# Local attention with its scores in two sets of PSUM banks, cache copies moved from the start to the middle, and a reordered tail, in one program

## The chip, the cores and the metric

The program runs on one core of a Trainium2 chip, in one launch. The metric is the device time of one execution in microseconds (us), lower is better. Five engines work side by side, each through its own queue in order: PE (TensorE, the matmuls; PEld is its weight load), DVE (VectorE), ACT (ScalarE), POOL (GpSimd) and SP (SyncE, which here only starts transfers). POOL also starts transfers, through a software queue of its own. All of them meet in SBUF (128 partitions) and in PSUM, whose banks take the matmuls' results.

## The reference

The reference is one inference step of a two-layer decoder on 1024 prompt tokens and 8 single decode tokens, width 1024, all in float32:

```
layer 0: x += norm(mix_A(norm(x)));  x += norm(mlp(norm(x)))    mix_A: gated linear attention + memory attention
shared:  k, v = split(norm(x) @ w_kv)                           4 kv heads of 64
layer 1: x += norm(mix_B(norm(x)));  x += norm(mlp(norm(x)))    mix_B: local attention + memory attention
mix_B:   q, qm = split(h @ w_in_b)
         s = q k^T / 8 + bias(distance), valid for 0 <= distance < 128
         m = max(max(s), sink);  p = exp(s - m) / (sum(exp(s - m)) + exp(sink - m));  o = p v
         decode token: the same over the 127 cached keys and its own
outputs: y of the prompt and of the decode tokens, the GLA states, the last 128 keys and values of the
         prompt, the decode caches shifted by one with the new key and value behind, the memory keys and values
```

The mlp is `square(relu(h @ w_up)) @ w_down` with 4096 hidden units. `norm` is a root-mean-square norm with a gain.

## The kernel before

The residual stream lies feature-major: 8 tiles of 128 features, with the 1032 tokens in three column chunks c = 0, 1, 2 of 384, 384 and 264 (`CH`). A projection in float32 is made of three matmuls on a high and a low part (`wh`, `wl`, `xh`, `xl`), so every weight is loaded (`ws`), cast on ACT (L152) and subtracted on DVE (L153) before PE uses it. The program's stages follow each other: load and norm of x with the first projections and the memory keys and values, linear attention, output projection, mlp of layer 0, projections of layer 1, attention of layer 1, output projection, mlp of layer 1. A scheduler writes each engine's queue once, from the program's order and from priorities (`tc.high_priority(n)` lets work be placed as if it had been written n instructions sooner); an engine never departs from that order.

**The start.** `load_split` (L1019) loads x of a chunk in four tiles `ld` of two feature tiles each. They are slices of one array `xT` of 1032 columns, so a partition's share of a transfer lies in two pieces of 1536 bytes (1056 for chunk 2). At once POOL starts a copy from DRAM to DRAM (L1785, `out_swa_ks`, 1016 KB): the old keys of the decode cache, shifted by one. L1786 does the same for the values at about 63 us. Nothing in the program reads these two results.

**The local attention.** `swa(t, i2)` is one unit: a pair of heads t (of 6) and two blocks of 128 queries, so 24 units. Its steps are: scores (PE, L1726, into a PSUM tile `sA` of two banks, of which the pool holds just one); addition of the bias and row maximum (DVE, L1730, four per unit); exponential with row sum (ACT, L1745, four); multiplication by the reciprocal (DVE, L1751); transposes (PE, L1758, into `sT`); copy to SBUF `pt` (ACT, L1760); product with the values (PE, L1769, into `sf`); copy to `q` (ACT, L1773). The units of t = 0 to 3 lie between the projections of `in_b`, which use two banks `mm`. After `in_b(4)` there are no projections until the output projection, so in the last eight units, (4,0) to (5,3), these two banks are free.

**The decode tokens** are a generator `swa_dec` with five steps: loads and own key; scores against the memory keys (L454, 32 matmuls); transposes and the scores against the cache (L1817); product with the memory values (L454 again) and with the cached values (L1846); copies of the results to `q` (L1862) and `qx` (L492). One step is taken ahead of each unit from (4,2) on. POOL starts its loads: cached keys and values, eight `in_mem_kT`, `vdec`, `dec_sink` and eight `in_mem_v`, the last of which go into the tiles of the memory keys. PE runs in order: a matmul that waits for one of these loads holds all that stand behind it.

**The end.** `down_plain(c)` (L980 on) makes the second projection of the last mlp for chunk c; DVE evicts each result with an addition (L996), `feed_last` squares it on ACT. `Residual.finish` then makes the norm: two last sums (L192), matmuls with a matrix of ones to add over partitions (L198, tile `sf`), logarithm and exponential on ACT (L205, L206), a refinement on DVE (L207 to L209) that leaves the factor `rf`. For each j of four, DVE then multiplies two feature tiles by `rf` (L320) and adds the residual `xall` (L322), and SP stores them to `yT` (L323). The tile `rf` comes from a pool of one buffer, so chunk 2's may be written only after chunk 1's last L320 has read it.

Of the kernel before, what the change touches and what calls it, by code (L numbers as in the profile page):

```python
# [16 lines left out]
P = 128  # L17
# [30 lines left out]
def hybrid_decoder_step(ctx: ExitStack, tc: tile.TileContext, A, O):  # L48
# [30 lines left out]
    xd = dram.tile([P, KT, NT], F32, tag="xd", name="xd")  # L79
# [35 lines left out]
    def first():  # L115
        return tc.high_priority(400)

# [145 lines left out]
    class Residual:  # L263
# [5 lines left out]
        def feed(self, m):  # L269
            if self.last:  # L270
                with first():
                    self.feed_last(m)
            elif m % 2:
                with first() if self.gnext is None else ExitStack():
                    self.sf.add(self.f[:, m - 1 : m + 1, :])
# [11 lines left out]
        def finish(self, bf):  # L287
            c0, n, f = self.c0, self.n, self.f
            rf = rp.tile([P, 384], F32, tag="rf", name=nm("rf"))[:, :n]
            rf2 = rf.unsqueeze(1).to_broadcast([P, 2, n])  # L290
            if self.last:
                with first():
                    self.sf.finish(rf)
            else:
                self.sf.finish(rf, bf)
                hl = xtiles(self.c)
                self.r = rtile(self.c)
# [6 lines left out]
            def load(j):  # L304
                if self.last:
                    got.append(xall[:, 2 * j : 2 * j + 2, :])
                    nc.gpsimd.dma_start(got[-1], self.xsrc[:, 2 * j : 2 * j + 2, c0 : c0 + n])
                    return
                xs = xsp[0].tile([P, 2, 384], F32, tag="xs", name=nm("xs"))[:, :, :n]
                with tc.high_priority(2 * WPRI):  # L310
                    nc.sync.dma_start(xs, self.xsrc[:, 2 * j : 2 * j + 2, c0 : c0 + n])
                got.append(xs)
# [4 lines left out]
            for j in range(4):  # L317
# [3 lines left out]
                if self.last:  # L321
                    TT(f[:, ks, :], f[:, ks, :], xs, ALU.add)  # L322
                    nc.sync.dma_start(O["yT"][:, ks, c0 : c0 + n], f[:, ks, :])  # L323
                    continue
# [5 lines left out]
                nc.scalar.dma_start(xd[:, ks, c0 : c0 + n], f[:, ks, :])  # L330
# [163 lines left out]
    def out_proj(l, make_o, src_pool, st, ff, xsrc, psum=True, oh0=None):  # L494
# [16 lines left out]
        def part(c, ms, pool):  # L511
            n = CH[c][1]
            if c not in FT:
                FT[c] = pool.tile([P, KT, n], F32, tag="f", name=nm("f"))
                R[c] = Residual(c, FT[c], G_MIXPOST + l, xsrc, gnext=G_FFNPRE + l)
# [101 lines left out]
    def mlp(l, X, ff):  # L617
# [45 lines left out]
        def square_mean(c):  # L663
            c0, n = CH[c]
            st = Stats(n, "sx")
            for j in range(4):
                xs = tmp3([P, 2, n])
                nc.sync.dma_start(xs, xd[:, 2 * j : 2 * j + 2, c0 : c0 + n])
                st.add(xs)
# [306 lines left out]
        def down_plain(c):  # L976
            hl = HL[c]
            c0, n = CH[c]
            R[c] = Residual(c, F[c], G_FFNPOST + l, xd, last=(l == 1), floor=X[c][1])
            for m in range(KT):  # L980
# [9 lines left out]
                with first():  # L990
# [48 lines left out]
    def load_x(between, use):  # L1039
        with tc.tile_pool(name="xload", bufs=7, reuse_waits="tile") as xl:  # L1040
            for c in range(3):
# [3 lines left out]
                load_split(xl, hl, A["xT"][:, :, c0 : c0 + n], n, r, G_MIXPRE, (2, 3, 4)[c] * 3 * KT * 384,  # L1045
# [78 lines left out]
    with ExitStack() as sl0:  # L1124
# [479 lines left out]
        with ExitStack() as so:  # L1604
# [30 lines left out]
            X = out_proj(0, make_o0, svp, so, ff, A["xT"], False, oh0)  # L1635
# [4 lines left out]
    with ExitStack() as sl1:  # L1640
# [8 lines left out]
        with ExitStack() as sa:  # L1649
# [63 lines left out]
            def swa(t, i2):  # L1713
# [6 lines left out]
                ps = psS().rearrange("p (j u k) -> p j u k", j=2, u=2)  # L1720
                row = Row()
                for u in range(2):
                    i = 2 * i2 + u
                    for j in range(2):
                        rows = slice(64 * j, 64 * j + 64)
                        row(nc.tensor.matmul(ps[:, j, u, lo[u] :], q[rows, t, i * P : i * P + P],  # L1726
                                             kf[rows, pr, i * P - P + lo[u] : i * P + P], start=True, stop=True))
                for u in range(2):
                    for j in range(2):
                        nc.vector.tensor_tensor_reduce(  # L1730
                            z[:, j, u, lo[u] :], ps[:, j, u, lo[u] :], bias[:, 2 * t + j, lo[u] :], 1.0,
# [43 lines left out]
            def swa_dec():  # L1775
# [8 lines left out]
                nc.gpsimd.dma_start(vc[WIN - 1 : WIN], vdec)  # L1784
                nc.gpsimd.dma_start(O["swa_ks"][:, : WIN - 1, :], A["swa_k_nat"][:, 1:, :])  # L1785
                nc.gpsimd.dma_start(O["swa_vs"][:, : WIN - 1, :], A["swa_v_nat"][:, 1:, :])  # L1786
# [80 lines left out]
            for t in range(6):  # L1867
# [6 lines left out]
                for i2 in range(NB // 2):  # L1874
                    if (t, i2) >= (4, 2):
                        next(dec, None)
# [22 lines left out]
def _arrays(inp):  # L1899
# [8 lines left out]
    a["xT"] = fm(np.concatenate([inp["x_prompt"][0], inp["x_sample"][:, 0]], 0))  # L1908
# [107 lines left out]
```

## Time and profile before

Three runs took 2204.39, 2208.44 and 2211.30 us; the median is 2208.44 us. The profiled execution took 2209.21 us, of which its span is 2207.4 us, so 1.8 us lie around the span. Its mean granted TensorE clock is 0.994.

| engine | busy us | share of the span |
|---|---|---|
| PE | 2152.1 | 97% |
| PEld | 2054.4 | 93% |
| DVE | 1504.0 | 68% |
| ACT | 1061.5 | 48% |
| POOL | 109.4 | 5% |

A row of a timeline reads: start in us, duration in us, engine, line of the kernel, operation, result<-operands, count, and in brackets how long the engine stood idle ahead of it and which engine's work ended that. A row of a table of windows gives the stretch, its length, the busy time of PE, PEld, DVE, ACT and POOL with their counts, the granted clock, the busy share of the DMA engines and the GB/s they moved.

### The profile page before, as it was taken

The page shows a single profiled execution, that of the slowest core. Times are in us where ns is not written, and L with a number is a line of the kernel's source. Part 1 is how long each engine was busy: PE and PEld are TensorE (multiplying, and loading weights), DVE is VectorE, ACT ScalarE, POOL GpSimd, SP SyncE. Part 2 cuts the span into 40 slices and gives each one's busy share as a digit, 9 for nine tenths or more (in the row PEclk, how much of TensorE's full clock was granted, in tenths as well). Part 3 has the DMA queues.
Part 4 walks back from the last instruction along what each step waited for, and adds up shares of the span by engine and source line. Part 5 has one row for each costly group of instructions (what it writes and reads, how often), then busy time and mean ns, then how long its engine had stood idle before and what let it go on. Part 6 is the DMA issues. An engine that isn't in the chain of part 4 may idle for free.

```text
span 2207.4 us, 40137 instructions
## 1 busy us (share of the span) xinstructions
PE 2152.1 (97%) x16250; PEld 2054.4 (93%) x16250; DVE 1504.0 (68%) x2811; ACT 1061.5 (48%) x2071; POOL 109.4 (5%) x123
## 2 busy tenths in 40 slices
PE   7999999999999999999999999799999999999996
PEld 5879999999999999999999778599999999999996
DVE  6656647768877777666478465647887776856557
ACT  6354536557644554334334365646654544433433
POOL 0002000000000002520000000100000000000010
PEclk9999999999999999999999999899999999999998
DMA  5512016543644459574334101324364337635422
GB/s 186 161 63 80 24 64 168 163 131 106 200 157 159 138 196 337 176 256 128 111 95 140 48 20 40 106 73 145 112 219 158 128 138 264 220 112 167 149 88 78
DMA packets 134687, 303.68 MB, mean 138 GB/s; under 512 B 11033, under 2 KB 65489, under 8 KB 134209
## 3 DMA queue, kind: packets, MB, share of 16 engines
q1 hardware_dynamic: 116736, 258.80, 36.0%
q0 software_dynamic: 7824, 29.44, 3.8%
q10 hardware_dynamic: 9936, 12.81, 1.6%
q8 instruction: 129, 2.11, 0.4%
q14 instruction: 62, 0.51, 0.1%
HBM read 213.57 MB, written 89.51 MB: 137 GB/s over the span
## 4 chain that ended last, share of the span: by engine, by line
PE 84%; DVE 4%; ACT 2%; DMA 2%; issue 1%; DVEq 0%; ACTq 0%
PE mm L248 15%; PE mx L248 7%; PE mx L756 6%; PE mx L758 6%; PE mx L757 6%; PE mx L921 4%; PE mx L923 4%; PE mx L922 4%; PE mm L756 3%; PE mm L758 3%; PE mm L757 3%; PE mm L922 2%; PE mm L921 2%; PE mm L923 2%; PE sx L921 1%; PE sf L922 1%
## 5 line engine op out<-in xcount | busy, mean ns | idle before, releaser
L152 ACT CAST wh<-ws 128x512 fp32r<-128x512 f32 (+1 forms) x262 | 188.3, 726 | 319.7 <-DVE ws L605 105.7
L153 DVE TENSOR_TENSOR wl<-ws,wh 128x512 fp32r<-128x512 f32 (+1 forms) x262 | 213.7, 822 | 122.8 <-ACT wh L152 121.7
L756 PE MATMUL mx<-xf,wh 128*128 128x258 f32 x1048 | 297.1, 283 | 0.0
L758 PE MATMUL mx<-xf,wl 128*128 128x258 f32 x1048 | 295.9, 282 | 0.0
L757 PE MATMUL mx<-xf,wh 128*128 128x258 f32 x1048 | 295.7, 282 | 0.0
L248 PE MATMUL mm<-xh,wh 128*128 128x384 f32 (+1 forms) x864 | 282.0, 326 | 0.8 <-ACT xh L152 0.5
L248 PE MATMUL mm<-xh,wl 128*128 128x384 f32 (+1 forms) x864 | 278.9, 323 | 0.0
L248 PE MATMUL mm<-xl,wh 128*128 128x384 f32 (+1 forms) x864 | 278.7, 323 | 0.0
L152 ACT CAST wh<-wr 128x1024 fp32r<-128x1024 f32 x98 | 103.0, 1051 | 315.3 <-PE sx L922 300.3
L153 DVE TENSOR_TENSOR wl<-wr,wh 128x1024 fp32r<-128x1024 f32 x98 | 119.8, 1223 | 173.7 <-ACT wh L152 173.7
L921 PE MATMUL mx<-sa,wh 128*128 128x258 f32 x784 | 221.6, 283 | 1.1 <-DVE aw L594 1.1
L922 PE MATMUL mx<-sa,wh 128*128 128x258 f32 x784 | 220.6, 282 | 0.0
L923 PE MATMUL mx<-sa,wl 128*128 128x258 f32 x784 | 220.5, 282 | 0.0
L757 PEld LDWEIGHTS mx<-xf,wh 128*128 128x128 f32 x1048 | 198.1, 189 | 0.4
L756 PEld LDWEIGHTS mx<-xf,wh 128*128 128x128 f32 x1048 | 197.7, 189 | 0.4
L758 PEld LDWEIGHTS mx<-xf,wl 128*128 128x128 f32 x1048 | 197.9, 189 | 0.0
L248 PEld LDWEIGHTS mm<-xh,wh 128*128 128x128 f32 x864 | 163.0, 189 | 10.8 <-issue 6.3
L248 PEld LDWEIGHTS mm<-xh,wl 128*128 128x128 f32 x864 | 162.6, 188 | 7.4 <-issue 5.4
L248 PEld LDWEIGHTS mm<-xl,wh 128*128 128x128 f32 x864 | 163.2, 189 | 6.5 <-issue 5.5
L921 PEld LDWEIGHTS mx<-sa,wh 128*128 128x128 f32 x784 | 147.5, 188 | 1.6 <-DVE aw L594 1.5
L922 PEld LDWEIGHTS mx<-sa,wh 128*128 128x128 f32 x784 | 148.4, 189 | 0.0
L923 PEld LDWEIGHTS mx<-sa,wl 128*128 128x128 f32 x784 | 148.1, 189 | 0.0
(542 smaller groups left out, 5749.6 us busy)
## 6 DMA issues: line engine op xcount, KB each, us to landing
ra<-awd SPq DMA_DIRECT2D x98, 516.0 KB, 3.9
ws<-in_w_up SPq DMA_DIRECT2D x64, 512.0 KB, 6.1
wr<-in_w_downb SPq DMA_DIRECT2D x56, 512.0 KB, 5.6
awd<-aw SPq DMA_DIRECT2D x26, 1032.0 KB, 6.8
awd<-am SPq DMA_DIRECT2D x28, 774.0 KB, 8.3
ws<-in_w_in_a SPq DMA_DIRECT2D x20, 512.0 KB, 3.6
xd<-f ACTq DMA_DIRECT2D x24, 384.0 KB, 4.8
ws<-in_w_out SPq DMA_DIRECT2D x16, 512.0 KB, 3.5
```

What stands on the lines that cost most here:

```text
L152: nc.scalar.copy(hi, src)
L153: (eng or nc.vector).tensor_tensor(lo, src, f32(hi), ALU.subtract)
L248: mm = nc.tensor.matmul(ps[:M, :n], w_[:, k, :M], x_[:, k, :], start=(i == 0), stop=(i == 3 * KT - 1))
L756: nc.tensor.matmul(ps, wh(k), xh, start=(k == 0), stop=False)
L757: nc.tensor.matmul(ps, wh(k), xl, start=False, stop=False)
L758: mm = nc.tensor.matmul(ps, wl(k), xh, start=False, stop=(k == n - 1))
L921: nc.tensor.matmul(ps, wh[:, q, ms], h, start=(jj == 0 and q == 0), stop=False)
L922: nc.tensor.matmul(ps, wh[:, q, ms], lo, start=False, stop=False)
L923: mm = nc.tensor.matmul(ps, wl[:, q, ms], h, start=False, stop=end)
```

## The change

There are three places. The line numbers of the changed kernel are 3 or 4 higher in the first third, and 9 to 12 higher from `swa` on; elsewhere the five queues hold the same instructions in the same order.

First, the input x and the DRAM copy `xd` of the residual stream become three arrays, one per chunk, so that a tile's share of a partition is one piece. The two shifting copies are put behind the load of `vdec` on POOL's queue, in the middle of the attention.

Second, in the last eight units every second one (i2 = 0 and 2) writes its scores into the two banks `mm`, one per head j, while the others keep `sA`. The decode steps are taken ahead of the units from (4,0) on.

Third, at the end chunk 2's factor has a tile of its own (`r0`), its work has a priority of 4000 in place of 400, and chunk 1's residual additions for j = 1 and 3 go from DVE to POOL.

```diff
...
     def first():
         return tc.high_priority(400)
+
+    def urgent(c):
+        return tc.high_priority(400 if c < 2 else 4000)
...
         def feed(self, m):
             if self.last:
-                with first():
+                with urgent(self.c):
                     self.feed_last(m)
...
-            rf = rp.tile([P, 384], F32, tag="rf", name=nm("rf"))[:, :n]
+            rf = rp.tile([P, 384], F32, tag="r0" if self.last and self.c == 2 else "rf", name=nm("rf"))[:, :n]
             rf2 = rf.unsqueeze(1).to_broadcast([P, 2, n])
             if self.last:
-                with first():
+                with urgent(self.c):
                     self.sf.finish(rf)
...
-                    nc.gpsimd.dma_start(got[-1], self.xsrc[:, 2 * j : 2 * j + 2, c0 : c0 + n])
+                    nc.gpsimd.dma_start(got[-1], self.xsrc[:, 2 * j : 2 * j + 2, :])
...
                 if self.last:
-                    TT(f[:, ks, :], f[:, ks, :], xs, ALU.add)
+                    eng = nc.gpsimd if self.c == 1 and j % 2 else nc.vector
+                    eng.tensor_tensor(f[:, ks, :], f[:, ks, :], xs, ALU.add)
                     nc.sync.dma_start(O["yT"][:, ks, c0 : c0 + n], f[:, ks, :])
...
-                with first():
+                with urgent(c) if l else first():
                     if c < 2:
                         TT(F[c][:, m, :], ps[:, :n], C(m, c)[:, :384], ALU.add)
...
-                load_split(xl, hl, A["xT"][:, :, c0 : c0 + n], n, r, G_MIXPRE, (2, 3, 4)[c] * 3 * KT * 384,
+                load_split(xl, hl, A[f"xT{c}"], n, r, G_MIXPRE, (2, 3, 4)[c] * 3 * KT * 384,
...
-                ps = psS().rearrange("p (j u k) -> p j u k", j=2, u=2)
+                if t >= 4 and i2 % 2 == 0:
+                    ps = [mmps(), mmps()]
+                else:
+                    ps = psS()
+                    ps = [ps[:, :512], ps[:, 512:]]
+                ps = [view(x, [P, 2, 256]) for x in ps]
...
-                        row(nc.tensor.matmul(ps[:, j, u, lo[u] :], q[rows, t, i * P : i * P + P],
+                        row(nc.tensor.matmul(ps[j][:, u, lo[u] :], q[rows, t, i * P : i * P + P],
                                              kf[rows, pr, i * P - P + lo[u] : i * P + P], start=True, stop=True))
...
-                nc.gpsimd.dma_start(vc[WIN - 1 : WIN], vdec)
-                nc.gpsimd.dma_start(O["swa_ks"][:, : WIN - 1, :], A["swa_k_nat"][:, 1:, :])
-                nc.gpsimd.dma_start(O["swa_vs"][:, : WIN - 1, :], A["swa_v_nat"][:, 1:, :])
+                own = nc.gpsimd.dma_start(vc[WIN - 1 : WIN], vdec)
+                for o, src in (("swa_ks", "swa_k_nat"), ("swa_vs", "swa_v_nat")):
+                    shift = nc.gpsimd.dma_start(O[o][:, : WIN - 1, :], A[src][:, 1:, :])
+                    tc.add_manual_dep(shift.ins, own.ins.name, NOSYNC, reason="behind the loads")
...
                 for i2 in range(NB // 2):
-                    if (t, i2) >= (4, 2):
+                    if t >= 4:
                         next(dec, None)
                     swa(t, i2)
```

What is left out of it passes the chunk's own array (`xd[c]`, `xT{c}`) where the slice stood, and cuts the inputs on the host into three arrays of the same values.

PE's queue where the eight units begin (`kf` keys, `q` queries, `sx` decode scores, `sT` transposes, `sf` products with the values) before:

```order
L1790 MATMUL sx_16442<-ident,kf 8x128 x2
L1769 MATMUL sf_16229<-pt_16227,vtok_14265 64x128 x8
L1726 MATMUL sA_16368<-kf,q 128x256 x4
L454 MATMUL sx_16505<-ar_16414,ar_16412 32x256
L1726 MATMUL sA_16461<-kf,q 128x256 x3
L1758 MATMUL sT_16349<-ident,z_16323 128x128 x6
L1726 MATMUL sA_16461<-kf,q 128x256
L1769 MATMUL sf_16358<-pt_16356,vtok_14265 64x128 x6
```

and in the changed kernel:

```order
L1778 MATMUL sf_16231<-pt_16229,vtok_14267 64x128 x8
L1735 MATMUL sA_16479<-kf,q 128x256 x2
L1735 MATMUL mm_16534<-kf,q 128x256
L1735 MATMUL mm_16535<-kf,q 128x256
L1735 MATMUL mm_16534<-kf,q 128x256
L458 MATMUL sx_16416<-ar_16327,ar_16325 32x256
L1735 MATMUL mm_16535<-kf,q 128x256
L1735 MATMUL sA_16609<-kf,q 128x256 x3
L1767 MATMUL sT_16399<-ident,z_16372 128x128 x6
L1735 MATMUL sA_16609<-kf,q 128x256
```

Before, the scores of unit (4,1) (`sA_16368`) and three quarters of those of (4,2) (`sA_16461`) stand ahead of the first transposes of unit (4,0), one tile after the other in the same two banks. Now those of (4,1) in `sA`, of (4,2) in the two `mm` tiles and three quarters of those of (4,3) in `sA` again stand there. The first decode scores (L454, now L458) keep their place beside them.

POOL's queue in the changed kernel around the two copies, with the semaphores that each transfer waits for (DMASW0 to DMASW7 are those of POOL's own transfers, taken in turn, so each transfer waits for the eighth before it):

```order
L1793 DMA ar_16328<-vdec_14257 1x8x256 [waits DMASW3_49]
L1795 DMA out_swa_ks<-in_swa_k_nat 8x2x16256 [waits DMASW4_49]
L1795 DMA out_swa_vs<-in_swa_v_nat 8x2x16256 [waits DMASW5_49]
L1805 MEMSET ar_16328 128x512
L1807 MEMSET ar_16328 128x256
L1818 DMA ar_16325<-in_dec_sink 128x1 [waits DMASW6_49]
L448 DMA ar_16325<-in_mem_v 128x512 [waits DMASW7_49,PE_49]
L448 DMA ar_16325<-in_mem_v 128x512 [waits DMASW0_49]
```

Before, `vdec` was followed by the two MEMSETs, `dec_sink` and the `in_mem_v` loads; the copies now stand ahead of these, and the last two of the eight `in_mem_v` wait for the copies' own semaphores.

DVE's queue at the end (`f_24597` is chunk 1, `f_24601` chunk 2) in the changed kernel:

```order
L195 TENSOR_TENSOR rf_25080<-tq_24969 128x264
L1000 TENSOR_TENSOR f_24601<-mx_25062,acc_21702 128x132
L1000 TENSOR_TENSOR f_24601<-mx_25062,acc_21704 128x132
L326 TENSOR_TENSOR f_24597<-f_24597,xall_24922 128x768
L323 TENSOR_TENSOR f_24597<-f_24597,rf_24913 128x768 x2
L210 TENSOR_TENSOR sf_25082<-sf_25082,rf_25080 128x264
L326 TENSOR_TENSOR f_24597<-f_24597,xall_24922 128x768
L211 SCALAR_TENSOR_TENSOR sf_25082<-sf_25082,rf_25080 128x264
L323 TENSOR_TENSOR f_24597<-f_24597,rf_24913 128x768
L212 SCALAR_TENSOR_TENSOR rf_25080<-sf_25082,rf_25080 128x264
L323 TENSOR_TENSOR f_24601<-f_24601,rf_25080 128x528 x2
```

Before, the sum of chunk 2 (L192, now L195) stood behind chunk 1's fourth multiplication (L320, now L323); now it is ahead of the last two evictions, and chunk 1's leftovers lie between the steps of chunk 2's refinement.

More of the change, by code (lines that the diff above doesn't have):

```diff
@@ L77, in hybrid_decoder_step @@
     nc.vector.memset(oneb, 1.0)
-    xd = dram.tile([P, KT, NT], F32, tag="xd", name="xd")
+    xd = [dram.tile([P, KT, n], F32, tag=f"xd{c}", name=f"xd{c}") for c, (_, n) in enumerate(CH)]
     srd = dram.tile([P, 6, NT], F32, tag="srd", name="srd")
@@ L310, in load @@
                 with tc.high_priority(2 * WPRI):
-                    nc.sync.dma_start(xs, self.xsrc[:, 2 * j : 2 * j + 2, c0 : c0 + n])
+                    nc.sync.dma_start(xs, self.xsrc[:, 2 * j : 2 * j + 2, :])
                 got.append(xs)
@@ L329, in finish @@
                     load(j + ahead)
-                nc.scalar.dma_start(xd[:, ks, c0 : c0 + n], f[:, ks, :])
+                nc.scalar.dma_start(xd[self.c][:, ks, :], f[:, ks, :])
                 if self.gnext is None:
@@ L514, in part @@
                 FT[c] = pool.tile([P, KT, n], F32, tag="f", name=nm("f"))
-                R[c] = Residual(c, FT[c], G_MIXPOST + l, xsrc, gnext=G_FFNPRE + l)
+                R[c] = Residual(c, FT[c], G_MIXPOST + l, xsrc[c], gnext=G_FFNPRE + l)
             for m in ms:
@@ L667, in square_mean @@
                 xs = tmp3([P, 2, n])
-                nc.sync.dma_start(xs, xd[:, 2 * j : 2 * j + 2, c0 : c0 + n])
+                nc.sync.dma_start(xs, xd[c][:, 2 * j : 2 * j + 2, :])
                 st.add(xs)
@@ L978, in down_plain @@
             c0, n = CH[c]
-            R[c] = Residual(c, F[c], G_FFNPOST + l, xd, last=(l == 1), floor=X[c][1])
+            R[c] = Residual(c, F[c], G_FFNPOST + l, xd[c], last=(l == 1), floor=X[c][1])
             for m in range(KT):
@@ L1634, in hybrid_decoder_step @@
                         make_o0(0, oh0)
-            X = out_proj(0, make_o0, svp, so, ff, A["xT"], False, oh0)
+            X = out_proj(0, make_o0, svp, so, ff, [A[f"xT{c}"] for c in range(3)], False, oh0)
         pmd.close()
@@ L1730, in swa @@
                         nc.vector.tensor_tensor_reduce(
-                            z[:, j, u, lo[u] :], ps[:, j, u, lo[u] :], bias[:, 2 * t + j, lo[u] :], 1.0,
+                            z[:, j, u, lo[u] :], ps[j][:, u, lo[u] :], bias[:, 2 * t + j, lo[u] :], 1.0,
                             sinks[:, 2 * t + j : 2 * t + j + 1], ALU.add, ALU.max,
@@ L1906, in fm @@
         return np.ascontiguousarray(x.T.reshape(KT, P, -1).transpose(1, 0, 2))
-    a["xT"] = fm(np.concatenate([inp["x_prompt"][0], inp["x_sample"][:, 0]], 0))
+    x = fm(np.concatenate([inp["x_prompt"][0], inp["x_sample"][:, 0]], 0))
+    for c, (c0, n) in enumerate(CH):
+        a[f"xT{c}"] = np.ascontiguousarray(x[:, :, c0 : c0 + n])
     a["memT"] = fm(inp["mem_prompt"][0])
```

## The prediction

> **What bounds the kernel now.** I began with the page's engine rows and its chain of waits.
>
> ```profile
> span 2207.4 us, 40137 instructions
> PE 2152.1 (97%) x16250; PEld 2054.4 (93%) x16250; DVE 1504.0 (68%) x2811; ACT 1061.5 (48%) x2071; POOL 109.4 (5%) x123
> PE 84%; DVE 4%; ACT 2%; DMA 2%; issue 1%; DVEq 0%; ACTq 0%
> ```
>
> PE is the bound nearly everywhere; 2207.4 − 2152.1 = 55.3 us of the span are without a matmul, and only these, and matmuls at a lower clock, can be saved by an edit that leaves PE's work as it is. The windows and timelines show three clusters of them, which are the three places of the change: the first 20 us, 1379 to 1441 us, and the last 20 us. I go through them in this order; each has its own bound.
>
> **The start.** The table of windows, then ACT's and PE's timelines and the transfers of the first 22 us:
>
> ```profile
> 0.00:10.00 10.00, 1.49 (x4) 0.22 (x4) 1.76 (x6) 3.14 (x4) 0.93 (x5) 1.00 0.79 270
> 10.00:20.00 10.00, 7.30 (x22) 2.72 (x23) 4.21 (x6) 4.56 (x10) 0.00 (x0) 1.00 0.73 246
> 20.00:30.00 10.00, 10.00 (x56) 5.83 (x56) 7.96 (x14) 8.72 (x18) 0.00 (x0) 1.00 0.61 187
> 11.70 1.04 ACT L152 CAST wh<-ws 128x1024 fp32r<-128x1024 f32 x1 [5.05 <-DMA ws<-in_w_in_a]
> 12.70 1.50 PE L1172 MATMUL mg<-ld,vtok 128*32 128x384 f32 x4 [6.38 <-DMA ld<-in_xT]
> q0 software_dynamic: 48, 1.04, 11.7%
> out_swa_ks<-in_swa_k_nat POOLq DMA_DIRECT2D x1, 1016.0 KB, 9.3
> ```
>
> In the first 20 us PE works 8.8, and the releasers of both long waits are transfers, the first weight and the second tile of x. The software queue's one transfer is the key copy; it took 11.7% of 16 engines over 22 us, so 0.117 × 22 = 2.6 us of all of them, ahead of or beside these loads. Taken away, ws and ld land up to 2.6 us sooner. The transfer engines were busy for 0.79 of the first 10 us and not for all of it, so 0.79 × 2.6 = 2.1 us is the share that I count; the longer pieces of x (the same bytes) add perhaps 0.4, an estimate between nothing and the 6.38 us of PE's wait. Term: **2.5 us**. Low bound 0.5: the casts of x on ACT and DVE could be the next limit, as ACT is 8.72 of 10 busy from 20 to 30. High bound 5: both waits 5.05 and 6.38 gone nearly whole. From 20 us on PE has no idle time, so what it gains is kept. `out_swa_vs` leaves the stretch at 63 us where PE is full anyway: nothing.
>
> **The middle.** PE's waits from 1378.8 to 1441.5 us, the stretch from the last projection to the output projection without a hole, and windows of it:
>
> ```profile
> PE sT L1758 <- DVE z L1751: 4.2, 4, 1.6
> PE sf L1769 <- ACT pt L1760: 3.2, 5, 1.2
> PE sA L1726 <- DVE sm L1730: 2.4, 3, 2.0
> PE sT L1758 <- DVE sm L1828: 2.0, 1, 2.0
> ...
> 1378.80:1441.50 62.70, 49.51 (x431) 32.92 (x430) 44.12 (x162) 38.87 (x108) 10.55 (x21) 0.89 0.29 96
> 1390.00:1400.00 10.00, 9.68 (x63) 5.36 (x64) 5.25 (x20) 5.27 (x18) 0.54 (x1) 0.59 0.13 45
> 1387.95 2.07 PE L1726 MATMUL sA<-kf,q 64*128 64x256 f32 x6 [1.95 <-DVE sm L1730]
> 1383.94 1.13 PE L1726 MATMUL sA<-kf,q 64*128 64x256 f32 x8
> ```
>
> No engine is full: PE 49.5, DVE 44.1 and ACT 38.9 of 62.7 us. PE stands because each unit is a chain (scores, maximum, exponential, normalising, transposes, copy, values) and the next unit's scores must wait until DVE has read the one `sA`. Of that kind is the wait of 1.95 us at 1387.95; behind it the clock is 0.59 and six score rows take 2.07 us where eight took 1.13.
>
> What each edit brings:
> - Two sets of score banks: the waits of `sA` on L1730, **2.4 us**, go. Low 0, if they return one unit later.
> - The slow stretch: at full clock its 9.68 us of matmuls would be 0.59 × 9.68 = 5.7, so up to 4.0 us. It follows the wait that goes, but a new one can bring it back; I take **2.5**.
> - With the scores of three units ahead, DVE and ACT find the next unit's work sooner, and the waits on `z` and `pt`, 4.2 + 3.2 = 7.4 us, shrink. The last units keep theirs, having nothing left to hide them. I take **3**; bounds 0 and 5.
> - New: the copies of the decode queries (L1803) and the result copy of unit (4,0) now stand on DVE and ACT behind unit (5,0)'s maxima and exponentials, so PE's L1817 and the values of (4,1), queued behind it, wait. The nearest row is the 2.0 us that PE stood for L1828: **−2**.
> - Decode steps two units sooner in the program move few rows on PE: both groups of L454 stand by unit (4,0)'s and (5,0)'s transposes as before. Nothing, as long as their loads have landed (below).
>
> Sum 2.4 + 2.5 + 3 − 2 = **5.9 us**. Bounds: −2 (only the new wait) and 4.0 + 2.4 + 5 = 11.4.
>
> The clock: by the Trainium skill, "TensorE: Matmul & The Clock Gate", Part 1, the clock halves after an idle window of about 3.4 us. The row shows half rate behind a wait of 1.95 us, shorter than that page's window, so the trace agrees in the halving but not in the length; by the page's length the 2.5 would have to come from something else and the middle would be 3.4.
>
> Where the copies go, POOL and its transfers:
>
> ```profile
> 1379.72 3.19 POOL L444 DMA_DIRECT2D ar<-in_mem_kT  x6
> 1387.70 0.57 POOL L1808 DMA_DIRECT2D ar<-in_dec_sink  x1 [2.89 <-DMA ar<-in_swa_kT]
> 1400.24 3.71 POOL L444 DMA_DIRECT2D ar<-in_mem_v  x7 [1.87 <-PE sx L454]
> ar<-in_swa_kT POOLq DMA_DIRECT2D x1, 1016.0 KB, 11.8
> ar<-in_mem_kT POOLq DMA_DIRECT2D x8, 256.0 KB, 9.3
> ar<-in_mem_v POOLq DMA_DIRECT2D x8, 256.0 KB, 4.6
> 1416.03 0.42 PE L454 MATMUL sx<-ar,ar 128*32 128x256 f32 x3
> ```
>
> The copies go out from about 1387.7, when in_swa_kT's landing lets POOL on. At 9.3 us each, side by side, they land by about 1399. In this stretch the engines move 45 GB/s from 1390 to 1400, so there is room. Queued behind on POOL's queue are dec_sink and the eight in_mem_v; these issued at 1397.8 to 1404 and landed by 1409, and PE read them at 1416. Five to seven us of slack cover the delay: nothing, with the price of a lost cover under the rivals.
>
> **The end.** Timelines of PE, DVE and ACT from 2187 us:
>
> ```profile
> 2193.45 1.25 PE L198 MATMUL sf<-rf,ones 128*128 128x264 f32 x2 [5.62 <-DVE rf L192]
> 2194.49 1.97 PE L198 MATMUL sf<-t,ones 128*128 128x264 f32 x4
> 2188.51 1.81 DVE L320 TENSOR_TENSOR f<-f,rf 128x768 f32<-128x768 f32 x2
> 2190.24 1.82 DVE L322 TENSOR_TENSOR f<-f,xall 128x768 f32<-128x768 f32 x2
> 2192.96 0.43 DVE L192 TENSOR_TENSOR rf<-tq 128x264 f32<-128x264 f32 x1
> 2188.62 0.42 ACT L280 ACTIVATE t<-f 128x264 f32<-128x264 f32 x1 [0.30 <-DVE f L996]
> 2196.91 0.42 ACT L206 ACTIVATE rf<-rf 128x264 f32<-128x264 f32 x1
> 2197.37 0.44 DVE L207 TENSOR_TENSOR sf<-sf,rf 128x264 f32<-128x264 f32 x1 [3.11 <-ACT rf L206]
> 2198.78 1.33 DVE L320 TENSOR_TENSOR f<-f,rf 128x528 f32<-128x528 f32 x2
> 2202.50 1.32 DVE L322 TENSOR_TENSOR f<-f,xall 128x528 f32<-128x528 f32 x2
> ```
>
> Before, DVE finishes chunk 1 (0.87 us per operation, from (2190.24 − 2188.51) / 2) up to L192, and only then PE sums chunk 2: 5.62 us of wait, then 3.0 us of cold matmuls, and 3.11 us of wait on DVE. Then eight operations of 0.62 us, 5.0 in all, to 2203.8, and 3.6 us of store and closing.
>
> Now L192 stands ahead of the last evictions, so the sums are done by about 2189.6 (last square of ACT at 2189.0, then two rows), ACT's two operations of 0.42 each by 2190.5. Of chunk 1, DVE has L322, L320 twice (to 2191.2), and between the refinement's three steps of 0.45 L322 and L320 once each: 5 × 0.87 + 3 × 0.45 = 5.7 from 2188.6, to 2194.3, and with the eight of chunk 2 to 2199.3. That would be 4.5 us less. But two additions of chunk 1 now run on POOL, and this is what two-operand work on POOL costs beside DVE:
>
> ```profile
> 880.05 19.65 POOL L237 TENSOR_TENSOR wf<-wf,gains 128x1024 f32<-128x1024 f32 x1 [4.64 <-DMA wf<-in_w_kv]
> 908.78 1.89 POOL L237 TENSOR_TENSOR wf<-wf,gains 128x1024 f32<-128x1024 f32 x1 [4.18 <-DMA wf<-in_w_in_b]
> 849.26 2.93 DVE L153 TENSOR_TENSOR sa<-ra,sa 128x1032 fp32r<-128x1032 f32 x1
> 896.72 1.22 DVE L153 TENSOR_TENSOR sa<-ra,sa 128x1032 fp32r<-128x1032 f32 x1
> 900.70 1.23 DVE L153 TENSOR_TENSOR wl<-wr,wh 128x1024 fp32r<-128x1024 f32 x1 [2.75 <-ACT wh L152]
> ```
>
> The same POOL operation takes 1.89 us alone and 19.65 when DVE works without a hole until 897.9, and then ends 1.8 us behind that. At 849.26 it is DVE that waits, 2.93 us in place of 1.22. The two exclude each other while both read two operands from SBUF. The Trainium skill says so in "SBUF — State Buffer", "Who interferes with whom": such a pair shares a read interface, and whoever starts first holds it for the whole instruction; the trace agrees.
>
> An addition of 768 takes 1.89 × 768/1024 = 1.4 us on POOL. The steps of the refinement read `sf` from PSUM, so POOL gets in beside L207 and beside L209, and DVE's next operation waits for the rest, 1.4 − 0.45 = 1.0 us each time. 2199.3 + 2 × 1.0 = 2201.3, against 2203.8: term **2.5 us**. High bound 4.5 (no exclusion), low −0.5: POOL gets in only when DVE is done at 2199.3, its two additions end at 2202.1, and chunk 2's four stores, queued behind chunk 1's last on SP, go out from there instead of 2200.7.
>
> **Sum.** 2.5 + 5.9 + 2.5 = 10.9 us from 2209.2, so 2198.3; I say **2198**. The profiled execution is 0.8 us above the median of the three runs, which themselves lie 7 us apart.
>
> **Rivals.**
> 1. The middle gives nothing: the wait moves from `sA` to L1817 and the values of (4,1), the slow clock returns behind it, and only start and end stay: 2209.2 − 5.0 = 2204. For it: each unit's chain is as long as before, and the waits on `z` and `pt` are larger than those on `sA`. Against it: DVE has 18.6 us of idle time there to be filled.
> 2. POOL is shut out at the end, as at 880: 2.5 + 5.9 − 0.5 = 7.9, so 2201. For it: that row. Against it: the refinement steps read PSUM, and 849 shows that POOL can win between two operations of DVE.
> 3. All comes: middle 11.4, end 4.5, start 2.5, 2191. For it: the waits and slow rows are all there to be had. Against it: the row at 849, and the order of the copies.
> 4. Slower: the copies hold up in_mem_v. If they run one after the other (9.3 each would be 1406.3; with in_swa_kT's 11.8 for the second, 1408.8) and the eight loads then at the pace of in_mem_kT, of which six went out from 1379.7 to 1382.9 and landed by about 1382.9 + 9.3 = 1392.2, so 12.5 us for six and 16.6 for eight, the last lands at 1425. PE reaches the second L454 group at about 1410 in the forecast, so it stands 15 us with the rest of (5,0) to (5,3) behind it, and 4.0 us more at the slow clock: middle 5.9 − 19 = −13, with start and end 5.0, in all 8 us slower, 2217. It decides once in_mem_v lands more than 11 us behind PE's need. Against it: the light load of 45 GB/s and the slack above.
>
> **Chances.** Forecast 0.55, rival 1 0.22, rival 2 0.10, rival 3 0.08, rival 4 0.05. A measurement here can tell about 0.3%, 6.6 us: faster means below 2201.8. Of the forecast nine tenths lie there, with rival 3 and half of rival 2: 0.50 + 0.08 + 0.05, and a little of rival 1: 0.65. Within 0.3%: 0.30. Slower: 0.05. The range runs from near rival 3 to past rival 1, since start and middle can both fall to their low bounds: 2189 to 2208; the forecast's own is 2194 to 2202.
>
> **What would show it.** Start: the first L152 (now L155) at about 9 instead of 11.70, and PE's first full window sooner. Middle: no wait of scores on L1730's successor, the granted clock of the ten us behind 1388 near 1, a wait of about 2 us at the decode scores, the output projection's steady run starting 6 us sooner counted from the last projection. A wait of L458 on in_mem_v would speak for rival 4. End: sums by 2190 counted with the old origin, DVE operations of 0.87 us stretched to about 1.9 beside two POOL rows of 1.4; POOL rows of 5 us or more that end behind DVE's last would be rival 2. I am wrong if the middle's stretch of 62.7 us does not shrink by at least 3, or if the end is not shorter by 1.5.

## The result

The changed kernel takes 2192.48 us (median of 6 runs, 2189.01 to 2196.33), the kernel before 2204.66 us (6 runs, 2203.33 to 2211.30): a ratio of 0.9935, with a 95% interval of 0.9921 to 0.9948. It is faster by 0.65%. The forecast was 2198 us in a range of 2189 to 2208. The profiled execution of the changed kernel took 2194.83 us, its span 2193.0 us, 14.4 us less than before.

To place these 14.4 us I compare the same matmul in both traces. All kernels here have 16250 of them. Four marks cut the span: the last projection matmul ahead of the eight units; matmul number 10501, which lies in the output projection behind them and is the same one in every kernel; the last matmul of the second mlp projection; the end of the span.

| us | to the last projection | middle | output projection and mlp | end | span |
|---|---|---|---|---|---|
| before | 1378.56 | 81.16 | 727.83 | 19.88 | 2207.43 |
| changed | 1375.29 | 73.92 | 726.25 | 17.55 | 2193.01 |
| difference | −3.27 | −7.24 | −1.58 | −2.33 | −14.42 |

The start, from the changed kernel's table of windows and the timelines of ACT and PE:

```profile
0.00:10.00 10.00, 3.10 (x9) 0.58 (x10) 3.28 (x8) 5.74 (x8) 0.20 (x4) 1.00 0.81 292
10.00:20.00 10.00, 10.00 (x40) 4.68 (x40) 6.48 (x12) 6.27 (x15) 0.00 (x0) 1.00 0.46 165
7.40 1.04 ACT L155 CAST wh<-ws 128x1024 fp32r<-128x1024 f32 x1 [1.03 <-DMA ws<-in_w_in_a]
8.40 1.50 PE L1176 MATMUL mg<-ld,vtok 128*32 128x384 f32 x4 [2.34 <-DMA ld<-in_xT]
```

The first weight is there at 7.40 instead of 11.70, and PE's second group starts at 8.40 instead of 12.70, 4.3 us sooner. In this pair of profiles about 1 us of that is lost on the way to the eight units.

The middle, from PE's waits between 1375 and 1433 us, a window, and the timelines of POOL, DVE and PE:

```profile
PE sf L1827 <- issue: 1.9, 1, 1.9
PE sf L1778 <- ACT pt L1769: 1.2, 1, 1.2
PE sT L1767 <- DVE z L1760: 0.9, 2, 0.6
PE sA L1735 <- DVE sm L1739: 0.7, 1, 0.7
...
1400.00:1410.00 10.00, 8.50 (x89) 5.22 (x81) 4.22 (x17) 2.34 (x6) 0.00 (x0) 0.53 0.01 2
1386.51 0.54 POOL L1805 MEMSET ar<- 128x512 f32 x1
1386.97 0.33 POOL L1807 MEMSET ar<- 128x256 f32 x1
1391.59 4.26 POOL L448 DMA_DIRECT2D ar<-in_mem_v  x8 [3.78 <-PE sx L458]
1397.93 0.16 DVE L1756 TENSOR_TENSOR sm<-sm,sm 128x4 f32<-128x4 f32 x1 [2.06 <-ACT z L1754]
1398.23 1.00 DVE L1813 COPY ar<-q 64x12 f32<-64x12 f32 x8
1399.73 1.18 PE L1827 MATMUL sf<-ar,ar 128*32 128x128 f32 x32 [1.86 <-issue]
```

The wait of scores on the maxima fell from 2.4 to 0.7 us; those of the transposes on `z` and of the products on `pt` fell from 7.4 to 2.1. A new one is longest, 1.86 us at the decode scores (L1827, L1817 before), and behind it the clock is 0.53 for ten microseconds. The waits that go and those that come are the forecast ones; why the new one stands there is the subject of the experiments.

The end, from the timelines of PE, DVE and POOL:

```profile
2176.18 1.32 PE L201 MATMUL sf<-t,ones 128*128 128x264 f32 x4
2178.25 2.29 POOL L326 TENSOR_TENSOR f<-f,xall 128x768 f32<-128x768 f32 x1 [58.00 <-DVE f L323]
2179.14 2.22 DVE L326 TENSOR_TENSOR f<-f,xall 128x768 f32<-128x768 f32 x1
2182.70 1.79 POOL L326 TENSOR_TENSOR f<-f,xall 128x768 f32<-128x768 f32 x1 [2.16 <-issue]
2182.94 2.74 DVE L323 TENSOR_TENSOR f<-f,rf 128x528 f32<-128x528 f32 x2
2188.08 1.31 DVE L326 TENSOR_TENSOR f<-f,xall 128x528 f32<-128x528 f32 x2
```

The sums are done within 2.0 us of the last matmul's start instead of 8.9. Beside each of POOL's two additions one DVE row is stretched: 2.22 us where 0.95 is usual, and 2.74 for a pair that takes 1.33.

### The profile page after: what moved, and what is told of

Its sections match the earlier page's. It is cut to its first block, busy times and chain, and to the rows that moved or that the text cites. A ratio compares the mean times of both kernels' runs of the same rounds, so it can differ in the third digit from the quotient of the medians.

```text
span 2193.0 us, 40134 instructions
## 1 busy us (share of the span) xinstructions
PE 2148.5 (98%) x16250; PEld 2053.3 (94%) x16250; DVE 1506.6 (69%) x2809; ACT 1060.4 (48%) x2071; POOL 107.8 (5%) x125
## 4 chain that ended last, share of the span: by engine, by line
PE 91%; DVE 3%; ACT 2%; DMA 2%; issue 1%; POOL 0%; SPq 0%; DVEq 0%; ACTq 0%
PE mm L251 17%; PE mx L251 8%; PE mx L760 6%; PE mx L762 6%; PE mx L761 6%; PE mx L925 4%; PE mx L927 4%; PE mx L926 4%; PE mm L762 3%; PE mm L760 3%; PE mm L761 3%; PE mm L925 2%; PE mm L926 2%; PE mm L927 2%; PE sx L925 1%; PE sf L926 1%
```

## The experiments

The table collects every profile, cut at the same marks. "Time" is the ratio to the kernel before with its interval, where it was timed.

| kernel | first mark | middle | mlp | end | span | time |
|---|---|---|---|---|---|---|
| before | 1378.56 | 81.16 | 727.83 | 19.88 | 2207.43 | 1 |
| changed | 1375.29 | 73.92 | 726.25 | 17.55 | 2193.01 | 0.9935 (0.9921 to 0.9948) |
| first place alone | 1373.20 | 88.11 | 726.24 | 19.89 | 2207.44 | 1.0004 (0.9992 to 1.0015) |
| second place alone | 1378.59 | 66.07 | 726.28 | 19.87 | 2190.81 | 0.9939 (0.9919 to 0.9958) |
| third place alone | 1375.80 | 82.19 | 726.29 | 17.54 | 2201.82 | 0.9988 (0.9975 to 1.0001) |
| changed, additions on DVE | 1375.13 | 72.69 | 726.28 | 16.42 | 2190.53 | 0.9940 (0.9917 to 0.9963) |
| changed, copies late | 1375.61 | 67.63 | 726.29 | 17.55 | 2187.06 | 0.9913 (0.9900 to 0.9927) |
| both of these | 1372.07 | 68.87 | 727.78 | 16.41 | 2185.13 | 0.9905 (0.9888 to 0.9921) |
| changed, copies behind dec_sink | 1374.07 | 67.84 | 726.30 | 17.56 | 2185.76 | one run, 2187.55 us |
| arrays alone | 1377.11 | 77.03 | 727.15 | 19.88 | 2201.17 | one run, 2202.99 us |
| banks alone | 1378.02 | 70.69 | 726.27 | 19.88 | 2194.86 | 0.9964 (0.9950 to 0.9978) |
| decode sooner alone | 1378.56 | 87.85 | 727.86 | 19.89 | 2214.16 | 1.0043 (1.0030 to 1.0056) |

The end repeats within 0.02 us, so differences there can be read to a tenth. The first mark varies by about 3 us between kernels that are alike up to it (third place alone: 1375.80, before: 1378.56), and the mlp lies between 726.2 and 727.9; there a difference of 1 to 3 us tells nothing by itself.

The middle varies most. Before, third place alone and arrays alone have the same order of instructions in it on PE, DVE, ACT and POOL, and it took 81.16, 82.19 and 77.03 us. The records of the granted clock show what differs. In the next table "PE idle" is the time of the middle without a matmul and "half clock" the time for which the granted clock was 0.5. "At most" is half of PE's busy time in it, the most that the half clock can have cost.

| us in the middle | whole | PE idle | half clock | at most |
|---|---|---|---|---|
| before | 81.16 | 13.2 | 13.7 | 6.4 |
| third place alone | 82.19 | 12.9 | 17.1 | 8.1 |
| arrays alone | 77.03 | 14.6 | 0 | 0 |
| first place alone | 88.11 | 14.1 | 34.1 | 14.0 |
| decode sooner alone | 87.85 | 14.9 | 20.5 | 10.1 |
| banks alone | 70.69 | 8.2 | 3.4 | 1.7 |
| changed | 73.92 | 7.6 | 10.2 | 4.4 |
| changed, additions on DVE | 72.69 | 7.6 | 6.8 | 3.0 |
| second place alone | 66.07 | 4.0 | 0 | 0 |
| changed, copies late | 67.63 | 4.4 | 3.4 | 1.7 |
| both of these | 68.87 | 4.3 | 6.8 | 3.4 |
| changed, copies behind dec_sink | 67.84 | 4.9 | 0 | 0 |

PE's idle time holds within 2 us among kernels that are alike in the middle; the half clock does not. It shows in the whole time too: the kernel before ran 50 more times beside the experiments, and its runs with a mean granted clock of 0.996 took 2202.7 us on average (9 runs), those with 0.991 took 2211.1 (4 runs).

### The first place alone

```diff
-    xd = dram.tile([P, KT, NT], F32, tag="xd", name="xd")
+    xd = [dram.tile([P, KT, n], F32, tag=f"xd{c}", name=f"xd{c}") for c, (_, n) in enumerate(CH)]
...
+                    tc.add_manual_dep(shift.ins, own.ins.name, NOSYNC, reason="behind the loads")
```

> The kernel before with the first place of the change alone: the three arrays of x and of its DRAM copy, and the two shifting copies behind the load of vdec. My theory, from the changed kernel's traces: PE's steady run starts 4.3 us sooner, about 1 us of that is lost again between 80 and 100 us, so the last projection before the eight units ends about 3.3 us sooner (1375.3 instead of 1378.6) and the whole takes 3 us less. The copies, now in the middle, cost nothing there: from the last projection to the output projection's steady run it stays at 62.7 us. Rival: the copies hold up dec_sink or in_mem_v in the order of before, the middle grows by 2 us or more and the whole gains 1 us or less.

The start came (PE's matmul 251 at 53.65 instead of 58.36 us, the first mark 5.4 us sooner), and all of it was lost again: the middle took 88.11 us instead of 81.16, and the ratio is 1.0004. The rival was right in its size. PE's waits in the middle of this kernel:

```profile
PE sA L1726 <- DVE sm L1730: 4.4, 4, 2.1
PE mm L248 <- DVE xl L153: 2.4, 1, 2.4
PE sf L1818 <- issue: 1.5, 1, 1.5
...
1402.18 1.33 PE L1726 MATMUL sA<-kf,q 64*128 64x256 f32 x8 [2.14 <-DVE sm L1730]
1407.09 1.94 PE L1818 MATMUL sf<-ar,ar 128*32 128x128 f32 x32 [1.48 <-issue]
```

None of them is a wait for a transfer, so the rival's reason, copies that hold up dec_sink or in_mem_v, is not seen. PE's idle time is 14.1 us where it was 13.2. What is longer is the time at the half clock, 34.1 us instead of 13.7; the decode scores take 1.94 us instead of 1.08 there. All ten runs show it, with mean clocks of 0.989 to 0.992 where the 20 runs of the kernel before beside them had 0.991 to 0.996. The order of instructions in the middle is another one than before, on PE, DVE and ACT: the decode scores start 33.9 us behind the first mark instead of 26.9.

### The second place alone

```diff
+                if t >= 4 and i2 % 2 == 0:
+                    ps = [mmps(), mmps()]
...
-                    if (t, i2) >= (4, 2):
+                    if t >= 4:
```

> The kernel before with the second place alone: every second one of the last eight units has its scores in the two projection banks, and the decode steps begin two units sooner. Theory: from the last projection to the output projection's steady run the changed kernel took 55.6 us where before took 62.7, and this part alone gives that, 7 us less in all, with the wait of about 1.9 us at the decode scores. Rival: a part of the 7 us comes from the copies or the earlier start, and this part alone gives 4 or less.

The middle took 66.07 us, 15.1 less than before and 7.9 less than in the changed kernel. Both theory and rival are wrong: nothing of the 7 us came from the copies, and the kernel that has them in the middle is 7.9 us longer there. The kernel with this place alone is as fast as the whole change. Waits and windows:

```profile
PE sA L1731 <- DVE sm L1735: 1.2, 1, 1.2
PE mm L248 <- DVE xl L153: 0.7, 1, 0.7
PE sf L1822 <- issue: 0.5, 1, 0.5
PE sf L1774 <- ACT pt L1765: 0.5, 1, 0.5
PE sT L1763 <- DVE z L1756: 0.4, 1, 0.4
...
1390.00:1400.00 10.00, 9.45 (x120) 6.22 (x118) 9.73 (x47) 9.14 (x35) 4.55 (x9) 1.00 0.41 129
1400.00:1410.00 10.00, 9.90 (x113) 6.50 (x111) 8.87 (x39) 6.68 (x22) 0.00 (x0) 1.00 0.30 111
```

From 1390 to 1410 PE is busy 19.4 of 20 us at the full clock, where the changed kernel had 0.53 in the second half; the decode scores wait 0.5 us instead of 1.86.

### The third place alone

```diff
-            rf = rp.tile([P, 384], F32, tag="rf", name=nm("rf"))[:, :n]
+            rf = rp.tile([P, 384], F32, tag="r0" if self.last and self.c == 2 else "rf", name=nm("rf"))[:, :n]
...
+                    eng = nc.gpsimd if self.c == 1 and j % 2 else nc.vector
```

> The kernel before with the third place alone: chunk 2's factor in a tile of its own, its work with priority 4000, and two of chunk 1's additions on POOL. Theory: from the end of the last matmul of the second mlp projection to the end of the span it takes 17.2 us instead of 19.6, so 2.3 less, and nothing else moves. Rival: the 1.7 us that the changed kernel gained between the output projection and the last matmul come from the new priorities, and this kernel is 4 us faster.

The end took 17.54 us, 2.34 less, as the theory has it. The mlp was 726.29 us as in the changed kernel, but the second place alone, which has none of the new priorities, shows 726.28 too. So the 1.58 us of the mlp do not belong to the change: in the profile of before PE waits 0.75 and 0.31 us there, at about 1860 us, and such waits are in some profiles and not in others. The time agrees in size, 0.9988, though its interval reaches 1.

### The changed kernel with the additions on DVE

```diff
-                    eng = nc.gpsimd if self.c == 1 and j % 2 else nc.vector
-                    eng.tensor_tensor(f[:, ks, :], f[:, ks, :], xs, ALU.add)
+                    TT(f[:, ks, :], f[:, ks, :], xs, ALU.add)
```

> The changed kernel with chunk 1's four residual additions all on DVE again. Theory, that POOL and DVE exclude each other: in the changed kernel two operations of DVE are longer by 1.3 and 1.4 us, 2.7 in all, beside POOL's rows of 2.29 and 1.79 us; two additions of 0.87 us on DVE cost 1.7, so this kernel is 0.9 us faster at the end than the changed one. Rival, that POOL's work is free beside DVE and the long rows have another cause: it is 1.7 us slower at the end, with the long rows still there.

The end took 16.42 us, 1.13 less than with POOL. The additions on DVE and what stands beside them:

```profile
2177.80 0.95 DVE L325 TENSOR_TENSOR f<-f,xall 128x768 f32<-128x768 f32 x1
2179.00 0.95 DVE L325 TENSOR_TENSOR f<-f,xall 128x768 f32<-128x768 f32 x1
2183.18 1.32 DVE L323 TENSOR_TENSOR f<-f,rf 128x528 f32<-128x528 f32 x2
```

With POOL idle no row is stretched. So at the end the new order and the tile of its own are worth 3.46 us (19.88 − 16.42), and moving two additions to POOL costs 1.13 of them. In the whole time 1 us is below what these runs can tell.

### The copies late, and both improvements

```diff
+            for o, src in (("swa_ks", "swa_k_nat"), ("swa_vs", "swa_v_nat")):
+                shift = nc.gpsimd.dma_start(O[o][:, : WIN - 1, :], A[src][:, 1:, :])
+                tc.add_manual_dep(shift.ins, zset[0].ins.name, NOSYNC, reason="behind the last memset")
```

Here `zset[0]` is the memset of unit (5,0), the last of POOL's work for the attention; the lines at the load of vdec are gone.

> The changed kernel with the two shifting copies behind POOL's memset for unit (5,0), thus behind all loads of the decode tokens, where POOL has nothing else to do until the residual loads of the last mlp. Theory: in the changed kernel the copies cost the middle some 8 us (it gained 15 us without them and 7 with them), because what stands behind them on POOL's queue was planned and done later. Here the middle takes 48 us instead of 55.6, as with the second place alone; start and end stay as in the changed kernel (about 4 and 2.3 us less than before); in all 20 to 22 us less than before. Rival: the gain of the second place alone hung on the copies being at the start, by the phase in which its loads arrive, and this kernel is no faster than the changed one.

> The same with chunk 1's additions all on DVE: theory 1.1 us less than with the copies late and the additions on POOL, the end at 16.4 us instead of 17.5, in all 21 to 23 us less than before. Rival: the two do not add up, and it is the same as that kernel within its interval.

With the copies late the middle took 67.63 us, 6.3 less than in the changed kernel, and the time is 0.9913 (0.9900 to 0.9927), against 0.9935 (0.9921 to 0.9948) of the changed kernel. The two intervals overlap by 0.0006, so the times alone only just part the two. In the middle the kernels that have the copies ahead of the memsets (73.92 and 72.69 us) lie above those that don't (66.07 to 68.87). The saving in span is 20.4 us, as forecast. With the additions on DVE as well the median is 2185.81 us, the ratio 0.9905 (0.9888 to 0.9921), the fastest of all kernels here, about 1% below before. That it beats the version with the late copies alone shows at the end (16.41 against 17.55 us), while the two intervals of the time overlap.

### The copies behind dec_sink

```diff
-                for o, src in (("swa_ks", "swa_k_nat"), ("swa_vs", "swa_v_nat")):
-                    shift = nc.gpsimd.dma_start(O[o][:, : WIN - 1, :], A[src][:, 1:, :])
-                    tc.add_manual_dep(shift.ins, own.ins.name, NOSYNC, reason="behind the loads")
...
-                nc.gpsimd.dma_start(dsink, A["dec_sink"])
+                own = nc.gpsimd.dma_start(dsink, A["dec_sink"])
+                for o, src in (("swa_ks", "swa_k_nat"), ("swa_vs", "swa_v_nat")):
...
```

> The changed kernel with the copies behind dec_sink and ahead of the in_mem_v loads, so that their traffic stays in the same stretch but the two memsets and dec_sink are ahead of them. Theory: the cost comes from the memsets (and the decode scores that need them), so the decode scores stand beside the transposes of (4,1) again, and the middle takes 51 us or less; what remains is the later in_mem_v. Rival: the traffic of 2 MB read and written itself, or the waits of in_mem_v behind it, is the cost, and the middle stays at 55 us or more.

The middle took 67.84 us: the theory's side, and better than its number. The timelines of POOL, DVE and PE:

```profile
1378.93 0.54 POOL L1802 MEMSET ar<- 128x512 f32 x1
1384.27 0.60 POOL L1817 DMA_DIRECT2D out_swa_ks<-in_swa_k_nat  x1 [0.89 <-DMA ar<-in_mem_kT]
1389.67 1.03 DVE L1810 COPY ar<-q 64x12 f32<-64x12 f32 x8
1391.26 1.08 PE L1827 MATMUL sf<-ar,ar 128*32 128x128 f32 x32 [0.51 <-issue]
```

The copies go out at the same time as in the changed kernel (1384.3 here, 1384.45 there), ahead of the same eight in_mem_v, and the middle is as short as in the kernels that have them elsewhere (66.07 to 68.87). So neither their traffic nor the waits of in_mem_v are the price. What differs is the order in which all engines' queues were written. Here DVE copies the decode queries (L1810) at 1389.67; in the changed kernel (its rows are under the result) it makes the copies (L1813) 8.6 us later, at 1398.23, after standing 2.06 us for ACT's exponentials, though both memsets were done by 1387.3. The memsets were ready 10.9 us before; they are not what the copies waited for. The copies stand late in DVE's queue, behind unit (5,0)'s maxima, because the scheduler writes the queues by what it reckons; with the two large copies ahead of the memsets on POOL it put everything that needs the memsets further back, on DVE, ACT and PE. That the reckoning did so is what I infer from the orders, and no run shows it; that the order differs, and that the memsets were ready long before their use, is in the rows.

### The arrays alone

The first place without the three lines on the copies.

> The kernel before with the three arrays of x and of its copy alone; the shifting copies stay at the start and at 63 us. Theory: of the 4.3 to 4.7 us by which PE's steady run started sooner with both, the copy's traffic is the larger part (2.6 us of all engines), so this one gives 1 to 2 us. Rival: the longer pieces are the larger part, 3 us or more.

PE's matmul 251 starts at 57.03 us. The five kernels with the old start have it between 57.34 and 58.36, so the arrays alone are worth 0.3 to 1.3 us, which one profile doesn't tell from nothing; PE's second group, at 12.07, lies within theirs (11.97 to 13.43). The six kernels with the whole first place have matmul 251 between 51.80 and 54.01, so the larger part is the copies', as the theory has it. The one run's 2202.99 us at a clock of 0.996 is what the kernel before takes at that clock. More telling is the middle. It has the order of before and took 77.03 us, 4.1 less:

```profile
1386.49 1.13 PE L1726 MATMUL sA<-kf,q 64*128 64x256 f32 x6 [1.95 <-DVE sm L1730]
1390.00:1400.00 10.00, 8.85 (x97) 5.59 (x94) 7.82 (x35) 6.38 (x20) 4.60 (x9) 1.00 0.45 135
```

The same wait of 1.95 us, and behind it the clock is 1.00 and six score rows take 1.13 us, where in the profile of before it was 0.59 and they took 2.07. So the slow stretch does not follow from the wait alone; the same program position can have it or not. Without it the middle is 4.1 us shorter although PE's idle time is 1.4 us longer; the most that before's 13.7 us at half clock can have cost is 6.4.

### The two halves of the second place

The two edits of the second place shown above, one each.

> The kernel before with the score banks alone: every second one of the last eight units in the two projection banks, the decode steps still ahead of (4,2) and later units. Theory: the banks carry most of the 13 to 15 us of the second place, since they take away what made a unit's scores wait for the one before: 8 us or more of it. Rival: without the decode steps moved, the decode work piles up behind the last units, and the banks alone give 4 us or less.

> The kernel before with the decode steps two units sooner alone, all scores in the one tile of two banks. Theory: it gives the rest, 3 to 6 us, as the decode matmuls fill PE's waits earlier and the last units have none behind them. Rival: with one tile for the scores PE's waits on it stay, and it gives nothing or is slower.

The banks alone gave 10.5 us of the middle's 15.1 and 0.9964 of the time: the theory. Against the 77.03 us of the same order at full clock it is 6.3; PE's idle time fell by 5.0. The decode steps alone made it slower, 87.85 us and 1.0043: the rival. PE's waits with the decode steps sooner and one tile of scores:

```profile
PE sT L1758 <- DVE z L1751: 8.4, 4, 3.4
...
1389.29 1.13 PE L1758 MATMUL sT<-ident,z 128*128 128x128 f32 x6 [3.37 <-DVE z L1751]
1390.00:1400.00 10.00, 9.55 (x92) 5.67 (x91) 4.74 (x24) 4.11 (x14) 2.02 (x4) 0.67 0.15 45
```

PE stands 3.37 us for the normalised rows of one unit, 8.4 in four waits where before had 4.2, and the clock is down behind the first. PE's idle time is 1.7 us longer than before in all, and 20.5 us instead of 13.7 are at half clock. I take it that with one score tile, decode work that is planned earlier is put ahead of units that then have no scores ready; which of its rows does that was not taken apart, and so it is not shown. The two edits need each other: −10.5 and +6.7 alone, −15.1 together.

## Why the prediction was right or wrong

**The time** was forecast 0.3% too high in the median, 5.5 us, inside the range; 4.5 of them come from the base, since the forecast counts from the profiled 2209.2 us and the median before is 2204.66; the direction and the size of the gain (10.9 forecast; 14.4 in the profile, 12.2 between the medians) were right. The end came out for the reasons told, the start for its reason with a size too small, the middle for other reasons.

**The start, 2.5 us.** The reason held: PE waited for the first weight and the second tile behind the copy. The term was too small: 4.3 us at PE's first groups and 3.3 at the first mark, and over all profiles, five with the old start and six with the new, the mean difference is 4.7 us at matmul 251 and 3.7 at the first mark. The step that was mis-sized is the 2.1 us for the copy, made of its share of the engines' time and a further discount of 0.79. With the arrays alone matmul 251 stood at 57.03 us, and with the copies gone as well 3.0 to 5.2 us sooner. Why that is more than the copy's 2.6 us of all engines stays open. The 0.4 for the arrays is not shown: they gave 0.3 to 1.3, within what such profiles differ.

**The middle, 5.9 us.** The sum came out at 7.2, by errors that cancelled; that it is near 5.9 is luck.
- The step "the copies ... nothing, with the price of a lost cover under the rivals" was wrong. Where the score banks are there they cost 4 to 8 us (73.92 and 72.69 against 66.07 to 68.87), of which about 3 are PE's idle time and the rest goes with the clock. In the old order they cost 7 us in the profiles (88.11 against 81.16), and there it is nearly all the half clock; the 1.0004 of the time says that they took back what the start had gained. I had looked for the cost in the landing of in_mem_v. That was on time as I had worked out: issued from 1391.6 to 1395.9, landing 4.2 us later, read by PE at 1409.9. Rival 4 had the right cause and the wrong mechanism: not a late transfer, but other engines' queues written in another order.
- The step "**−2**" for the new wait was right in place and size (1.86 us at L1827), but I took it as a price of the score banks. It is the copies' price: without them there the decode scores wait 0.5 us.
- The terms for the banks were too small. For the waits 2.4 + 3 = 5.4 stood against 9.2 us of idle time that PE lost in the second place alone (13.2 to 4.0). For the slow clock 2.5 stood against up to 6.4, all of which the profile of before happened to have and this one did not. The two together account for the 15.1 measured. The waits on `z` and `pt` shrank from 7.4 to 0.9 in the second place alone, not by 3: the end of the eight units did not keep its waits, as I had thought.
- "Decode steps two units sooner in the program move few rows on PE ... Nothing" was wrong. I read it off the changed kernel's order, which had the copies in it. Alone that edit costs 6.7 us, beside the banks it brings 4.6 (70.69 − 66.07), 4.2 of it in PE's idle time.

**The clock.** I took 2.5 of 4.0 us for the slow stretch, as if it hung on the wait of 1.95 us. The arrays alone show the same wait and no slow stretch, and the clock's records show why. In each of the twelve traces all changes of the granted clock lie on one grid of 3.41 us, to within 4 ns, and the grid lies otherwise against the program in each. In the profile of before the whole wait falls into one piece of that grid, 1384.53 to 1387.94 us, in which PE was busy 33% of the time, and the clock falls at its end. With the arrays alone the grid cuts the wait in two: PE is busy 56% of the piece from 1382.30 to 1385.72 and 74% of the next, and the clock stays. Over all twelve traces, every piece at full clock in which PE is busy 43% or less is followed by half clock, no piece with 59% or more is, and between these both occur. So my step went by the length of the wait, where PE's share of a piece of the grid decided, and with it the chance of where the grid lies. The Trainium skill, "TensorE: Matmul & The Clock Gate", Part 1, says that the window in which activity is judged runs freely and does not begin with the kernel's work. The grid in these traces agrees with it.

**The end, 2.5 us.** 2.33, and by the steps as told: the sums ready early, POOL in beside the refinement's steps twice, two DVE rows longer by 1.3 and 1.4 us (I had 1.0 each), POOL's rows 2.29 and 1.79 us where I had 1.4 alone. Had I worked out the sum without POOL, 4.5 us, and set the two additions' 1.7 against it, I would have seen that moving them is worth nothing there: measured 3.46 without POOL, 2.33 with it.

**The rest, 1.58 us** between the output projection and the last matmul, was in no term, and is no effect of the change: kernels with none of the new priorities show it, and the fastest kernel does not.

**Rivals.** Of rival 1 the wait at L1817 and the slow clock behind it happened as told (0.53 from 1400 to 1410), but the middle gained 7 us all the same, since the second place was worth twice what I had given it. Rival 2 (POOL shut out) did not happen: POOL got in within the first step of the refinement. Rival 3's 2191 was near in time, with another make-up.

## What to carry to other kernels

- Undo each place of a change alone, and do each alone. Here the first place alone is worth nothing, the second alone is worth the whole, and the sum of the parts hid a loss of 4 to 8 us in the middle that the place of the two copies caused; with the copies moved and the additions back on DVE the kernel is about 1% faster than before in place of 0.65%.
- Where a scheduler writes the queues, a large transfer on a queue can have two prices: the time of the transfer, and the place where the scheduler then puts what depends on the work queued behind it (the second as far as the orders here show). Put transfers that nobody waits for behind the last work that somebody waits for.
- Before moving an operation to a second engine, see whether the two can run beside each other: the rows in which both were busy (19.65 us for 1.89) told it here.
- Where PE stands often for a microsecond or two, split a stretch into PE's idle time and the time at half clock before comparing two profiles. Here kernels alike in the middle differed by 5 us through the second alone.

## What was not expected of the hardware

The granted clock changes only on a grid of 3.41 us that lies otherwise in each execution, and a piece of it in which PE is busy 43% or less costs the full clock for the next one to five pieces of the middle (3.4 to 17.1 us). So a wait of 1.95 us is followed by ten microseconds at a clock of 0.50 in one execution and not in another with the same order of instructions, and the runs of the kernel before lie, on average, between 2202.7 us where their clock is 0.996 and 2211.1 where it is 0.991. Kernels that are alike up to the first mark reach it 3 us apart, and waits of about 1 us in the last mlp are there in some profiles and not in others. Below 3 us, then, a profile can be read for a stretch whose time repeats, as the end's does to 0.02 us, and not for the whole.
